# Selection shares with the queries on the partitions, small transfers on ScalarE's queue, key loads behind the queries

## The chip, the core and the metric

The kernel runs on one core of a Trainium2 chip. The core has five engines that run side by side and wait for each other by semaphores: TensorE (PE, matrix products and transposes, with its weight loads shown as PEld), VectorE (DVE), ScalarE (ACT), GpSimd (POOL) and SyncE (SP, which here only issues transfers). SP and ACT each have a queue of their own for transfers; both feed the same 16 DMA engines. Every engine runs its instructions in order. The metric is the device time in microseconds, median over runs.

## The reference

One step of a decoder layer: an RMS norm and a joint input projection, then two groups of heads side by side (native sparse attention, and a gated DeltaNet recurrence over 16 chunks of 128 tokens), then the output projection. There are 2048 prompt tokens and 8 x 4 sample tokens, 8 query heads in 2 key/value groups, head size 64. The part that the change touches is the choice of blocks in the sparse attention: probabilities over 127 compressed keys are summed into 32 blocks and over the four heads of a group, and the 8 best blocks are attended to.

```python
s = jnp.einsum('bqhgd,bchd->bhgqc', q_raw, ck).astype(jnp.float32) * scale
p = jax.nn.softmax(jnp.where(cmask, s, MASK_VALUE), axis=-1) * cmask
o_cmp = jnp.einsum('bhgqc,bchd->bqhgd', p.astype(cv.dtype), cv)
overlap = jnp.maximum(ov, 0).astype(jnp.float32) / CMP_LEN
imp = jnp.einsum('bhgqc,cn->bhqn', p, overlap)
imp = jnp.where(blk <= q_blk[:, None], imp + FORCE_BONUS * forced, MASK_VALUE)
_, idx = lax.top_k(imp, n_sel)
```

The chosen blocks then have their own softmax over rotated keys (`o_slc`), a window of 512 keys a third one (`o_win`), and the three are mixed by gates.

## The kernel before, in words

`project` computes the projections in 3-pass split precision, `gdn` the recurrence with the compression of keys as filler, `nsa` the sparse attention, and an output projection follows. Instructions are traced in the order of the code, but a planner with a simulated timeline sets the order on every engine and queue. So the work of `nsa` for its first unit is interleaved with the last steps of `gdn`, and transfers can be issued in another order than in the code.

**Projection of the keys.** For each of 5 groups of 416 tokens the keys are turned to rows in four pieces (`tk`, L406), copied by ACT to `er` (L408, two buffers under the tag `cx`) and written out (L411, L414) from SP's queue.

**The recurrence.** Step `n` of `recur` makes, in turn, `pk`, `pqs`, `pv`, `pS` (state update by DVE, L829) and `po` (L833). `tokens` loads `v` (one buffer) and `kq` for each step from SP's queue.

**Units of the sparse attention.** A unit is 512 queries of one key/value group: 4 x 2 = 8 units, in `units`. `stream` makes a unit's scores and values item by item (`pss` L1445/1446, exponential on ACT L1487, `O` L1578). Beside it the loop at the end of `nsa` advances `prepare` of the next unit at a rate that finishes in time; it also calls `load_q` for the next unit and, at units 0, 2 and 4, `load_k` for the keys of the next 512 (seven transfers, together 2.3 MB, behind the matmul `here[0]`). `QHL` and `QHM` hold the queries per group, so those of the next unit can only be loaded when the unit before the running one has used them up; `QRM` and `QRL` hold the unrotated queries and exist once.

**`prepare`** has two lists. `A` makes the compressed scores and the choice: `cmax` (row maxima from `psc`, L1321), `cmax_end` (maxima turned to rows by `rows_of`, and sent into row 97 of `QRM`), `csc` (probabilities `pT`, keys on the partitions, queries on the free axis), `share` (sums over keys by a matmul with ones, `psl` L1337; sent to DRAM, `Ld`, L1339, and read back 16 to a partition, L1341), `inverse` (reciprocal on DVE, L1344; to DRAM, L1346, and back, L1347), `share2` (block sums `psp` L1353 times the reciprocals), `select` (`psi`, sum over heads and turn, L1359; the 8 best) and `sel_rows` (mask rows into `QHM`, and a copy to the three other heads, L1372). `B` makes the exact maxima of the block and window scores (`smax`, `psm` L1379; `wmax`, `psw` L1394; `wmax0`). Both are interleaved: after entry `j` of `A`, `(j + 1) / n` of `B` has been emitted; `gap` entries of `A` only make room. `max_end` and `max_rows` close a unit with the maxima's rows in `QHM`, which the unit's own `pss` reads.

Most transfers of `nsa` go through the helper `dma` (shown as L1218) or `nc.sync.dma_start`, both SP's queue. `next_windows` copies two caches of 2 MB from DRAM to DRAM on ACT's queue at the start of units 2 and 4 (L1209).

Of the kernel before, what the change touches and what calls it, by code (L numbers as in the profile page):

```python
# [104 lines left out]
class K:  # L105
# [105 lines left out]
    def project(self):  # L211
        nc, tc, i, o = self.nc, self.tc, self.i, self.o
        with ExitStack() as st:
# [178 lines left out]
            for g in range(NG):  # L392
                gs = slice(g * GW, (g + 1) * GW)
                kr = ev.tile([128, 2, GW], F32, tag="kr", name="kr", bufs=3)
                for j in range(2):
                    ps = fm(*kw[j], g)
                    nc.scalar.activation(kr[:, j, :], ps, AF.Copy)
                    if j == 0:
                        rope(kr[:, 0, :], g, True)
                    hi, lo = hilo(kr[:, j, :])  # L400
                    nc.sync.dma_start(self.kh[:, 32 * j:32 * j + 32, gs], hi)
                    nc.sync.dma_start(self.kl[:, 32 * j:32 * j + 32, gs], lo)
                for c in range(4):
                    tp = pt.tile([128, 2, 128], F32, tag="tp", name="tk")
                    for j in range(2):
                        nc.tensor.transpose(tp[:104, j, :], kr[:, j, 104 * c:104 * c + 104], self.ident)  # L406
                    e = ev.tile([128, 256], F32, tag="cx", name="er")
                    nc.scalar.activation(e[:104].rearrange("p (c j d) -> p j c d", c=4, j=2), tp[:104].rearrange("p j (c d) -> p j c d", c=4), AF.Copy)  # L408
                    t0 = g * GW + 104 * c
                    t1 = min(t0 + 104, SEQ)  # L410
                    nc.sync.dma_start(tok(6)[t0:t1, :], e[0:t1 - t0, 0:128])  # L411
                    a = max(t0, 1536)
                    if a < t1:
                        nc.sync.dma_start(tok(10)[a - 1536:t1 - 1536, :], e[a - t0:t1 - t0, 128:256])  # L414
                    if t1 < t0 + 104:
                        nc.sync.dma_start(tok(7), e[t1 - t0:104, 0:128])
                        nc.sync.dma_start(self.wks, e[t1 - t0:104, 128:256])
# [219 lines left out]
    def gdn(self):  # L637
        nc, tc, i, o = self.nc, self.tc, self.i, self.o
        with self.gst as st:
# [143 lines left out]
                nc.scalar.activation(Y[0:64, :, 64:128], pq[:, 1], AF.Copy, scale=-1.0)  # L783

            kqr, kd4, vb4, O4, ZS = {}, {}, {}, {}, {}

            FB, FS, FL, FR = self.fills

# [18 lines left out]
            def recur(n):  # L807
# [22 lines left out]
                po = bank([128, 4, 128], "po")  # L830
                O4[n] = (self.gp if n % 2 else wk).tile([128, 4, 128], F32, tag="o4", name="o4", bufs=1)
                for h in range(4):
                    nc.tensor.matmul(po[:, h, :], QK[n][:, h, :], V[:, h, :], start=True, stop=True)  # L833
                    nc.vector.scalar_tensor_tensor(O4[n][:, h, :], ob[:, h, :], ed[:, h, n:n + 1], po[:, h, :], op0=ALU.mult, op1=ALU.add)
                yield

# [374 lines left out]
    def nsa(self):  # L1211
        nc, tc, i, o = self.nc, self.tc, self.i, self.o
        with ExitStack() as st:
# [4 lines left out]
            dma = lambda t, s, at=None: self.behind(nc.sync.dma_start(t.bitcast(F32), s), at)  # L1218
            units = [(qs, h) for qs in self.nsa_blocks for h in range(2)]
            nq = units[-1][0] + 1  # L1220

# [80 lines left out]
            def prepare(u):  # L1302
# [15 lines left out]
                def cmax(s):  # L1318
                    ps = X([128, 4, 128], "psc")
                    for g in range(4):  # L1320
                        nc.tensor.matmul(ps[:, g, :], QRM[0:97, g, 128 * s:128 * s + 128], CXL[0:97, h, 0, qs, :], start=True, stop=True)  # L1321
                    nc.vector.tensor_reduce(out=m[:, :, s], in_=ps, axis=AX.X, op=ALU.max)

                def cmax_end():
                    nc.vector.tensor_scalar(m, m, -(2.0 ** 60), -1.0, op0=ALU.max, op1=ALU.mult)
                    dma(QRM[97:98], rows_of(m.rearrange("p g s -> p (g s)"), 16))

                def csc(g):
                    ps = X([128, 512], "psr") if (qs, h) == units[0] else pS.tile([128, 512], F32, tag="s", name="psr")
# [2 lines left out]

                def share():

                    ps = X([128, 512], "psl")
                    for g in range(4):
                        nc.tensor.matmul(ps[32 * g:32 * g + 32, :], self.ones[:, 0:32], pT[g], start=True, stop=True, tile_position=(0, 32 * g))  # L1337
                    nc.vector.tensor_scalar(rl, ps, 1e-30, None, op0=ALU.max)
                    nc.sync.dma_start(u["Ld"][0], rl[0:128:32, :])  # L1339
                    u["r16"] = ns.tile([128, 16], F32, tag="r16", name="r16", bufs=1)  # L1340
                    nc.sync.dma_start(u["r16"], u["Ld"][0].rearrange("g (a x) -> (g a) x", x=16))  # L1341

                def inverse():
                    nc.vector.reciprocal(u["r16"], u["r16"])  # L1344
                    d = self.dram.tile([4, 512], F32, name="rd")
                    nc.sync.dma_start(d.rearrange("g (a x) -> (g a) x", x=16), u["r16"])  # L1346
                    nc.sync.dma_start(rl, d.unsqueeze(1).to_broadcast([4, 32, 512]))  # L1347

                def share2():

                    ps = X([128, 512], "psp")
                    for g in range(4):
                        nc.tensor.matmul(ps[32 * g:32 * g + 32, :], self.ovl, pT[g], start=True, stop=True, tile_position=(0, 32 * g))  # L1353
                    nc.vector.tensor_tensor(out=rl, in0=ps, in1=rl, op=ALU.mult)

                def select():
                    ps = X([128, 4, 32], "psi")
                    for s in range(4):
                        nc.tensor.matmul(ps[:, s, :], rl[:, 128 * s:128 * s + 128], self.gsum, start=True, stop=True)  # L1359
                    nc.vector.tensor_tensor(out=imp, in0=ps, in1=bon, op=ALU.add)  # L1360
                    t8 = ns.tile([128, 4, 8], F32, tag="t8", name="t8")
                    for s in range(4):
                        nc.vector.max(t8[:, s, :], imp[:, s, :])
                        nc.vector.match_replace(imp[:, s, :], t8[:, s, :], imp[:, s, :], 1e30)
                    nc.vector.tensor_scalar(imp, imp, 1e29, -BIG, op0=ALU.is_lt, op1=ALU.mult)

                def sel_rows():
                    tp = X([32, 512], "tsel")
                    for s in range(4):
                        nc.tensor.transpose(tp[:, 128 * s:128 * s + 128], imp[:, s, :], self.ident)  # L1370
                    nc.scalar.activation(QHM[64:96, 0], tp, AF.Copy)
                    nc.sync.dma_start(QHM[64:96, 1:4].bitcast(F32), QHM[64:96, 0:1].bitcast(F32).to_broadcast([32, 3, 512]))  # L1372

                def smax(s, g, a):
                    qt = 4 * qs + s
                    b = min(a + 4, qt + 1)
                    diag = b == qt + 1
                    ps = X([128, 512], "psm")
                    nc.tensor.matmul(ps[:, 0:128 * (b - a)], QHL[:, g, 128 * s:128 * s + 128], key(KHH, 0, h, a, b), start=True, stop=not diag)  # L1379
# [31 lines left out]
                    nc.vector.tensor_scalar(wm, wm, -1.0, None, op0=ALU.mult)  # L1411

                def max_rows():
                    dma(QHM[96:98], rows_of(wm.rearrange("p a g s -> p (a g s)"), 32))

                gap = lambda n: [None] * n
                A = [lambda s=s: cmax(s) for s in range(4)] + [cmax_end] + gap(8) + [lambda g=g: csc(g) for g in range(4)]
                A += [share] + gap(5) + [inverse] + gap(7) + [share2] + [select] + gap(2) + [sel_rows]
                B = []
                for s in range(4):  # L1420
                    for g in range(4):
# [5 lines left out]
                for j, f in enumerate(A):  # L1427
                    if f:
                        f()
                        yield  # L1430
                    e = (j + 1) * len(B) // n
                    for f in B[k:e]:
                        f()
                        yield
# [4 lines left out]
                max_rows()  # L1439
                yield  # L1440

            prepare.steps = lambda u: 16 + 32 + 16 * u["qs"] + (4 if u["qs"] else 0)
# [174 lines left out]
            here = [None]  # L1617
            for what, k in stream():
                if k in copies:
                    self.next_windows(*copies.pop(k), here[0])  # L1620
                if gen is None and k + 1 < len(units) and k + 1 not in U:
                    U[k + 1] = load_q(*units[k + 1])
                    if k % 2 == 0 and units[k][0] + 1 < nq:
                        load_k(units[k][0] + 1, here[0])
                    gen = prepare(U[k + 1])
                    done, steps, total = 0, 0, prepare.steps(U[k + 1]) + self.nx
                    rate = total / max(1, count(units[k][0]) - self.ny)
# [15 lines left out]
    mc = 9.0, 0.0  # L1643
    npre = 1
    jpre = 0
    nx, ny, npt, nos = 10, 4, 8, 9
    nd = 2, 3, 5, 8
    nb = 1.1, 0.5
# [411 lines left out]
```

## Time and profile before

| | |
|---|---|
| median of 3 runs | 2344.72 us (2339.41 to 2345.8) |
| profiled execution | 2345.71 us, span 2343.6 us |
| granted TensorE clock, mean | 0.957 of full speed |
| PE busy | 2179.5 us, 93% |
| DVE busy | 1278.6 us, 55% |
| ACT busy | 796.1 us, 34% |
| POOL busy | 766.4 us, 33% |
| transfers | 248.12 MB, of which 194.53 MB on SP's queue (q1) and 17.72 MB on ACT's (q10) |

Times in the trace are us from the span's start. A matmul in single precision shows as two records, each with a weight load. Matmuls are pipelined and their ends are modelled, so a busy PE is not PE at its peak. [...] The projections lie in about 0 to 790, the recurrence in 790 to 1216 (with the first unit's preparation in its last part), the stream of the sparse attention in 1216 to 2050, and the rest behind that.

### The profile page before, as it was taken

The numbers are of one execution on the slowest core, as the hardware profiler recorded it, in microseconds if no ns is written. First come the engines' busy times: TensorE is split into PE (matmuls) and PEld (weight loads), VectorE is DVE, ScalarE is ACT, GpSimd is POOL, SyncE is SP. The second block draws the span as 40 slices with busy tenths as digits, with TensorE's granted clock in tenths as the row PEclk, the third lists the DMA queues.
The fourth block names the chain that finished last, engine by engine and source line by source line (L and its number), as shares of the span: only waits on it lengthen the run. The fifth ranks groups of instructions, "written<-read, shape, count | busy, mean of one in ns | idle before, by whom it ended". The sixth has DMA issues, their size and how long they took to land. (4 is left out here: it accounts for less than half of the span.)

```text
span 2343.6 us, 36127 instructions
## 1 busy us (share of the span) xinstructions
PE 2179.5 (93%) x13339; PEld 1667.9 (71%) x13340; DVE 1278.6 (55%) x2660; ACT 796.1 (34%) x1688; POOL 766.4 (33%) x957
## 2 busy tenths in 40 slices
PE   6999999999999999996798969969999999999998
PEld 6999889999999788996674534535455553477765
DVE  5200246656420376566545758857778786845532
ACT  5311233332222143443353223324343434522221
POOL 4023211111200105413142334536473655422742
PEclk9999999999999899998798979989999998999999
DMA  7342421233541655437545433242222002374552
GB/s 214 108 109 62 119 86 63 77 63 73 148 141 63 187 153 157 146 106 164 133 117 97 102 76 80 51 113 48 38 48 37 21 9 57 108 229 153 195 188 93
DMA packets 304467, 248.12 MB, mean 106 GB/s; under 512 B 106039, under 2 KB 260835, under 8 KB 301987
## 3 DMA queue, kind: packets, MB, share of 16 engines
q1 hardware_dynamic: 282923, 194.53, 32.2%
q0 software_dynamic: 7424, 33.56, 4.3%
q10 hardware_dynamic: 13944, 17.72, 2.5%
q8 instruction: 105, 1.72, 0.3%
q14 instruction: 71, 0.58, 0.1%
HBM read 173.60 MB, written 74.42 MB: 106 GB/s over the span
## 5 line engine op out<-in xcount | busy, mean ns | idle before, releaser
L1588 POOL TENSOR_TENSOR pt<-pt 128x512 f32<-128x512 f32 (+3 forms) x332 | 320.5, 977 | 372.9 <-PE O L1578 160.5
L1487 ACT ACTIVATE pt<-pss 128x512 f32<-128x512 f32 (+3 forms) x544 | 254.5, 494 | 369.6 <-PE pss L1446 195.1
L1578 PE MATMUL O<-pt,V 128*64 128x512 f32 (+3 forms) x1088 | 242.9, 526 | 10.3 <-DVE pt L1497 10.3
L1382 DVE TENSOR_REDUCE bm<-psm 128x8 f32<-128x512 f32 (+3 forms) x320 | 189.6, 603 | 93.2 <-PE psm L1379 79.2
L1445 PE MATMUL pss<-qhl,khh 128*128 128x512 f32 (+3 forms) x544 | 218.5, 407 | 1.2 <-ACT pt L1487 0.6
L1445 PEld LDWEIGHTS pss<-qhl,khh 128*128 128x128 f32 x544 | 105.2, 194 | 137.5 <-issue 98.0
L1446 PE MATMUL pss<-qhm,klm 98*128 98x512 f32 (+3 forms) x544 | 192.5, 362 | 4.1 <-DMA qhl<-rl 3.8
L261 PE MATMUL ps<-xhi,whi 128*128 128x416 f32 x880 | 190.0, 357 | 0.0
L261 PE MATMUL ps<-xhi,wlo 128*128 128x416 f32 x880 | 189.7, 355 | 0.0
L261 PE MATMUL ps<-xlo,whi 128*128 128x416 f32 x880 | 187.1, 353 | 0.0
L261 PEld LDWEIGHTS ps<-xhi,whi 128*128 128x128 f32 x880 | 166.1, 190 | 13.0 <-issue 4.7
L1379 PE MATMUL psm<-khh,qhl 128*128 128x512 f32 (+3 forms) x320 | 128.7, 415 | 45.2 <-DMA qhl<-ql 26.1
L261 PEld LDWEIGHTS ps<-xhi,wlo 128*128 128x128 f32 x880 | 165.6, 189 | 2.0
L261 PEld LDWEIGHTS ps<-xlo,whi 128*128 128x128 f32 x880 | 165.4, 189 | 2.1
L1497 DVE TENSOR_TENSOR pt<-pt,caps 128x128 f32<-128x128 f32 x349 | 139.8, 419 | 20.0 <-ACT pt L1487 18.7
L1588 DVE TENSOR_TENSOR pt<-pt 128x512 f32<-128x512 f32 (+3 forms) x148 | 122.5, 837 | 38.2 <-PE O L1578 20.0
L466 DVE SCALAR_TENSOR_TENSOR acc<-cx,wc,acc 128x416 f32<-128x416 f32 (+1 forms) x180 | 123.9, 689 | 4.6
L1379 PEld LDWEIGHTS psm<-khh,qhl 128*128 128x128 f32 x320 | 62.1, 198 | 82.7 <-issue 45.6
L1446 PEld LDWEIGHTS pss<-qhm,klm 98*128 98x128 f32 x544 | 106.8, 197 | 15.2 <-DMA qhl<-rl 4.6
L1578 PEld LDWEIGHTS O<-pt,V 128*64 128x64 f32 x1088 | 55.5, 137 | 85.0 <-issue 33.3
L239 DVE TENSOR_TENSOR wlo<-wraw,whi 128x1024 fp32r<-128x1024 f32 x30 | 36.5, 1254 | 143.2 <-ACT whi L238 94.8
L1396 DVE TENSOR_REDUCE ww<-psw 128x1 f32<-128x512 f32 (+3 forms) x128 | 80.9, 632 | 28.6 <-PE psw L1395 28.0
(506 smaller groups left out, 4148.7 us busy)
## 6 DMA issues: line engine op xcount, KB each, us to landing
kq<-qkvt SPq DMA_DIRECT2D x64, 256.0 KB
qkvt<-acc SPq DMA_DIRECT2D x60, 208.0 KB
wraw<-w_in SPq DMA_DIRECT2D x24, 512.0 KB
xt<-x_prompt SPq DMA_DIRECT2D x16, 512.0 KB
m<-mx SPq DMA_DIRECT2D x16, 512.0 KB
x<-x_prompt ACTq DMA_DIRECT2D x16, 512.0 KB
out<-y SPq DMA_DIRECT2D x16, 512.0 KB
qh<-hi SPq DMA_DIRECT2D x20, 208.0 KB
```

The source lines that it names most:

```text
L239: nc.vector.tensor_tensor(out=wlo[:, :, c:c + m], in0=raw, in1=whi[:, :, c:c + m].bitcast(F32), op=ALU.subtract)
L261: nc.tensor.matmul(ps, x, y, start=(k == 0), stop=(k == 23))
L466: nc.vector.scalar_tensor_tensor(acc[:, :n], cx[:, j:j + n], wc[:, j, c:c + 1], acc[:, :n], op0=ALU.mult, op1=ALU.add)
L1379: nc.tensor.matmul(ps[:, 0:128 * (b - a)], QHL[:, g, 128 * s:128 * s + 128], key(KHH, 0, h, a, b), start=True, stop=not diag)
L1382: nc.vector.tensor_reduce(out=bm[:, s, g, 2 * a:2 * b], in_=ps[:, 0:128 * (b - a)].rearrange("p (n k) -> p n k", k=64), axis=AX.X, op=ALU.max)
L1396: nc.vector.tensor_reduce(out=ww[:, g, s, 0:1], in_=ps[:, 0:128 * (e - a)], axis=AX.X, op=ALU.max)
L1445: nc.tensor.matmul(ps, lhs1, r1, start=True, stop=False)
L1446: nc.tensor.matmul(ps, lhs2, r2, start=False, stop=True)
L1487: last = nc.scalar.activation(pt[:, c0:c1], ps[:, c0:c1], AF.Exp)
L1497: last = nc.vector.tensor_tensor(out=x, in0=x, in1=caps[:, int(nm == "neglow")], op=ALU.min)
L1578: mm = nc.tensor.matmul(O[64 * gg:64 * gg + 64, c0:c1], val, W[j][gg][:, c0:c1], start=(n == 0), stop=(n == N - 1), tile_position=(0, 64 * ...
L1588: (nc.gpsimd if e == "p" else nc.vector).tensor_tensor(out=acc[gg][:, c0:c1], in0=acc[gg][:, c0:c1], in1=W[j][gg][:, c0:c1], op=ALU.add)
```

## The change

Four things are edited. The shares are made with the queries on the partitions: `pT` slices become the stationary side against the block overlap, DVE sums the 32 block shares of a head (each key's overlaps add up to one, so this is the softmax sum), takes the reciprocal, multiplies, and sums over heads; the sums still go to `Ld` for the final merge, by a transpose and a copy in `share_rows`. The rows of maxima, the copies of the mask and the key rows in `project` are issued by ACT. `load_k` is called 8 events of the stream later (`kd`), and entries of `B` start after entry 6 of `A` (`bs`). The first `psc` is ordered behind the recurrence's `po` of step 6 and the first `psm` behind that of step 7 (`pst`), in order only, without a wait.

```diff
-                    nc.sync.dma_start(tok(6)[t0:t1, :], e[0:t1 - t0, 0:128])
+                    nc.scalar.dma_start(tok(6)[t0:t1, :], e[0:t1 - t0, 0:128])
...
-                        nc.sync.dma_start(tok(10)[a - 1536:t1 - 1536, :], e[a - t0:t1 - t0, 128:256])
+                        nc.scalar.dma_start(tok(10)[a - 1536:t1 - 1536, :], e[a - t0:t1 - t0, 128:256])
...
+                        mm = nc.tensor.matmul(ps[:, g, :], QRM[0:97, g, 128 * s:128 * s + 128], CXL[0:97, h, 0, qs, :], start=True, stop=True)
+                        if (qs, h, s, g) == (*units[0], 0, 0):
+                            self.tc.add_manual_dep(mm.ins, self.po[self.pst].ins.name, mybir.DependencyInfo(mybir.DependencyClass.NoSync, mybir.DependencyReason.DATA), reason="not ahead of its data")
...
-                    dma(QRM[97:98], rows_of(m.rearrange("p g s -> p (g s)"), 16))
+                    dma(QRM[97:98], rows_of(m.rearrange("p g s -> p (g s)"), 16), e=nc.scalar)
...
-                    ps = X([128, 512], "psl")
+                    ps = X([128, 4, 4, 32], "psp")
                     for g in range(4):
-                        nc.tensor.matmul(ps[32 * g:32 * g + 32, :], self.ones[:, 0:32], pT[g], start=True, stop=True, tile_position=(0, 32 * g))
...
+                        for s in range(4):
+                            nc.tensor.matmul(ps[:, s, g, :], pT[g][:, 128 * s:128 * s + 128], self.ovl, start=True, stop=True)
+                    u["l"] = ns.tile([128, 2, 4, 4], F32, tag="r16", name="r16", bufs=1)
+                    l, r = u["l"][:, 0], u["l"][:, 1]
+                    nc.vector.tensor_reduce(out=l, in_=ps.rearrange("p s g b -> p g s b"), axis=AX.X, op=ALU.add)
+                    nc.vector.tensor_scalar(l, l, 1e-30, None, op0=ALU.max)
+                    nc.vector.reciprocal(r, l)
+                    t = rl.rearrange("p (s g b) -> p s g b", s=4, g=4)
+                    nc.vector.tensor_tensor(out=t, in0=ps, in1=r.rearrange("p g s -> p s g").unsqueeze(3).to_broadcast([128, 4, 4, 32]), op=ALU.mult)
+                    nc.vector.tensor_reduce(out=imp, in_=t.rearrange("p s g b -> p s b g"), axis=AX.X, op=ALU.add)
+
+                def share_rows():
+                    tp = X([16, 128], "tl")
+                    nc.tensor.transpose(tp, u["l"][:, 0].rearrange("p g s -> p (g s)"), self.ident)
+                    r = ns.tile([32, 128], F32, tag="rows", name="lrows")
+                    nc.scalar.activation(r[:16], tp, AF.Copy)
+                    nc.sync.dma_start(u["Ld"][0].rearrange("g (s q) -> (g s) q", q=128), r[:16])
 
                 def select():
-                    ps = X([128, 4, 32], "psi")
-                    for s in range(4):
-                        nc.tensor.matmul(ps[:, s, :], rl[:, 128 * s:128 * s + 128], self.gsum, start=True, stop=True)
-                    nc.vector.tensor_tensor(out=imp, in0=ps, in1=bon, op=ALU.add)
+                    nc.vector.tensor_tensor(out=imp, in0=imp, in1=bon, op=ALU.add)
...
-                    nc.sync.dma_start(QHM[64:96, 1:4].bitcast(F32), QHM[64:96, 0:1].bitcast(F32).to_broadcast([32, 3, 512]))
+                    nc.scalar.dma_start(QHM[64:96, 1:4].bitcast(F32), QHM[64:96, 0:1].bitcast(F32).to_broadcast([32, 3, 512]))
...
-                    dma(QHM[96:98], rows_of(wm.rearrange("p a g s -> p (a g s)"), 32))
+                    dma(QHM[96:98], rows_of(wm.rearrange("p a g s -> p (a g s)"), 32), e=nc.scalar)
...
-                A += [share] + gap(5) + [inverse] + gap(7) + [share2] + [select] + gap(2) + [sel_rows]
+                A += [share] + gap(2) + [select] + gap(2) + [sel_rows, share_rows]
...
-                    e = (j + 1) * len(B) // n
+                    e = max(0, j - self.bs) * len(B) // (n - 1 - self.bs)
...
+                if coming:
+                    coming[0] -= 1
+                    if coming[0] < 0:
+                        load_k(coming[1], here[0])
+                        coming = None
...
-                        load_k(units[k][0] + 1, here[0])
+                        coming = [self.kd, units[k][0] + 1]
...
+    bs = 6
+    pst = 6
+    kd = 8
```

`smax` gets the same kind of order on its first matmul, behind `self.po[self.pst + 1]`; `self.po[n]` is the last `po` matmul of step `n`.

## Rows read from the trace of the kernel before

**Rows 1.** Waits of PE over the span: total us, times, longest us.
```profile
PE psm L1379 <- DMA qhl<-ql: 26.1, 4, 16.1
PE psm L1379 <- DMA mx<-mg: 16.0, 1, 16.0
PE psc L1321 <- DMA QRM<-qh: 14.8, 1, 14.8
PE pS L828 <- DVE S L829: 13.5, 2, 13.2
...
PE O L1578 <- DVE pt L1497: 10.3, 11, 3.6
PE psr L1446 <- DMA QRM<-rows: 9.7, 1, 9.7
PE tk L406 <- ACT er L408: 5.8, 2, 4.9
PE th L430 <- ACT er L408: 5.3, 2, 5.1
...
PE pss L1446 <- DMA qhl<-rl: 3.8, 1, 3.8
```
**Rows 2.** Stretches: length, busy us by engine, granted clock, DMA share, GB/s.
```profile
1077.60:1085.00 7.40, 7.38 (x44) 6.85 (x45) 3.03 (x7) 1.94 (x7) 0.77 (x3) 0.58 0.83 162
1144.10:1162.50 18.40, 18.39 (x103) 14.32 (x104) 10.90 (x37) 4.51 (x17) 1.31 (x5) 0.51 0.29 87
1249.00:1254.00 5.00, 5.00 (x17) 3.32 (x19) 1.70 (x4) 2.35 (x5) 0.00 (x0) 0.50 0.08 5
1369.50:1381.50 12.00, 12.00 (x40) 6.89 (x41) 4.11 (x11) 3.48 (x7) 1.76 (x2) 0.53 0.14 26
...
1055.00:1162.00 107.00, 75.53 (x674) 63.57 (x674) 57.47 (x175) 32.54 (x117) 24.30 (x44) 0.79 0.68 149
```
**Rows 3.** SP's queue in order of time: start, length, line, transfer, count.
```profile
1130.31 0.56 SPq L1339 DMA_DIRECT2D Ld<-rl  x1
...
1142.08 0.34 SPq L1341 DMA_DIRECT2D r<-Ld  x1
...
1245.40 0.61 SPq L1218 DMA_DIRECT2D QRM<-rows  x1
...
1338.08 1.38 SPq L1218 DMA_DIRECT2D khh<-kh  x2
...
1361.16 0.30 SPq L1218 DMA_DIRECT2D qhl<-ql  x1
...
1547.39 6.64 SPq L1250 DMA_DIRECT2D V<-svd  x1
```
**Rows 4.** DVE in order of time, in brackets the idle time and its releaser.
```profile
1143.63 0.25 DVE L1344 RECIPROCAL r<-r 128x16 f32<-128x16 f32 x1 [14.49 <-DMA r<-Ld]
```
**Rows 5.** ACT in order of time, its issues of transfers as ACTq.
```profile
1237.07 0.27 ACT L1290 ACTIVATE rows<-tm 16x128 fp32r<-16x128 f32 x1 [2.75 <-PE tm L1288]
...
1337.80 0.73 ACTq L1209 DMA_DIRECT2D out<-cache_win_k  x1
```
**Rows 6.** PE in order of time, neighbours of one line merged.
```profile
1248.78 1.65 PE L1446 MATMUL psr<-QRM,cxl 98*128 98x512 f32 x3 [9.66 <-DMA QRM<-rows]
...
1268.24 1.07 PE L1353 MATMUL psp<-pc,ovl 128*32 128x512 f32 x8
...
1271.35 1.08 PE L1359 MATMUL psi<-gsum,rl 128*128 128x32 f32 x8 [0.75 <-DVE rl L1354]
```
**Rows 7.** Instructions on `psi` and `psl`: ns min/median/max, first and last start.
```profile
L1359 PEld LDWEIGHTS psi<-gsum,rl x64: 186/192/333, 1155.2 to 1916.7; 128*128 128x128 f32 x64
...
L1338 DVE TENSOR_SCALAR rl<-psl x8: 677/684/692, 1120.4 to 1875.7; 128x512 f32<-128x512 f32 x8
```
**Rows 8.** DMA queues from 1340 to 1344: packets, MB, share of 16 engines.
```profile
q10 hardware_dynamic: 81, 1.32, 82.3%
q1 hardware_dynamic: 36, 0.07, 4.8%
```

More of the change, by code (lines that the diff above doesn't have):

```diff
@@ L785, in gdn @@
             kqr, kd4, vb4, O4, ZS = {}, {}, {}, {}, {}
+            self.po = {}
             FB, FS, FL, FR = self.fills
@@ L832, in recur @@
                 for h in range(4):
-                    nc.tensor.matmul(po[:, h, :], QK[n][:, h, :], V[:, h, :], start=True, stop=True)
+                    self.po[n] = nc.tensor.matmul(po[:, h, :], QK[n][:, h, :], V[:, h, :], start=True, stop=True)
                     nc.vector.scalar_tensor_tensor(O4[n][:, h, :], ob[:, h, :], ed[:, h, n:n + 1], po[:, h, :], op0=ALU.mult, op1=ALU.add)
@@ L1217, in nsa @@
             pM = st.enter_context(self.pool(name="pnM", bufs=self.pb3[2], space=PSUM))
-            dma = lambda t, s, at=None: self.behind(nc.sync.dma_start(t.bitcast(F32), s), at)
+            dma = lambda t, s, at=None, e=nc.sync: self.behind(e.dma_start(t.bitcast(F32), s), at)
             units = [(qs, h) for qs in self.nsa_blocks for h in range(2)]
@@ L1320, in cmax @@
                     for g in range(4):
-                        nc.tensor.matmul(ps[:, g, :], QRM[0:97, g, 128 * s:128 * s + 128], CXL[0:97, h, 0, qs, :], start=True, stop=True)
+                        mm = nc.tensor.matmul(ps[:, g, :], QRM[0:97, g, 128 * s:128 * s + 128], CXL[0:97, h, 0, qs, :], start=True, stop=True)
+                        if (qs, h, s, g) == (*units[0], 0, 0):
+                            self.tc.add_manual_dep(mm.ins, self.po[self.pst].ins.name, mybir.DependencyInfo(mybir.DependencyClass.NoSync, mybir.DependencyReason.DATA), reason="not ahead of its data")
                     nc.vector.tensor_reduce(out=m[:, :, s], in_=ps, axis=AX.X, op=ALU.max)
@@ L1333, in share @@
                 def share():
-                    ps = X([128, 512], "psl")
+                    ps = X([128, 4, 4, 32], "psp")
                     for g in range(4):
-                        nc.tensor.matmul(ps[32 * g:32 * g + 32, :], self.ones[:, 0:32], pT[g], start=True, stop=True, tile_position=(0, 32 * g))
-                    nc.vector.tensor_scalar(rl, ps, 1e-30, None, op0=ALU.max)
-                    nc.sync.dma_start(u["Ld"][0], rl[0:128:32, :])
-                    u["r16"] = ns.tile([128, 16], F32, tag="r16", name="r16", bufs=1)
@@ L1341, in share @@
[L1341 to L1354, printed above, removed]
+                        for s in range(4):
+                            nc.tensor.matmul(ps[:, s, g, :], pT[g][:, 128 * s:128 * s + 128], self.ovl, start=True, stop=True)
@@ L1378, in smax @@
                     ps = X([128, 512], "psm")
-                    nc.tensor.matmul(ps[:, 0:128 * (b - a)], QHL[:, g, 128 * s:128 * s + 128], key(KHH, 0, h, a, b), start=True, stop=not diag)
+                    mm = nc.tensor.matmul(ps[:, 0:128 * (b - a)], QHL[:, g, 128 * s:128 * s + 128], key(KHH, 0, h, a, b), start=True, stop=not diag)
+                    if (qs, h, s, g) == (*units[0], 0, 0):
+                        self.tc.add_manual_dep(mm.ins, self.po[self.pst + 1].ins.name, mybir.DependencyInfo(mybir.DependencyClass.NoSync, mybir.DependencyReason.DATA), reason="not ahead of its data")
                     if diag:
@@ L1440, in prepare @@
                 yield
-            prepare.steps = lambda u: 16 + 32 + 16 * u["qs"] + (4 if u["qs"] else 0)
+            prepare.steps = lambda u: 15 + 32 + 16 * u["qs"] + (4 if u["qs"] else 0)
             def scores(ps, lhs1, lhs2, r1, r2):
@@ L1616, in nsa @@
             gen, nxt, done, total = None, None, 0, 0
-            here = [None]
+            here, coming = [None], None
             for what, k in stream():
```

## The prediction

> **What bounds the kernel now.** I read the busy times first: TensorE (PE) is busy 2179.5 of the span's 2343.6 us, so at most 164 us can come from its idle time, and a faster engine elsewhere gives nothing by itself. Next, the waits of PE, longest in total [rows 1]: about half of that idle time stands in a few long waits, nearly all for data that the diff touches. [...] Last, the queue of SyncE (SP) and the engine in front of PE [rows 3, 4, 5], because a wait that is named after a transfer can be one for the transfer's turn. The profiled execution took 2345.71 us, 1 us over the median of 2344.72; the sum is made against 2345.71.
>
> The waits by stage, all from rows 1: **A**, in the projection of the keys (5.8 + 5.3, `tk` and `th` for `er`); **B**, the first compressed maximum for its queries (14.8); **C**, the shares' round trip (13.2 of 13.5, in one piece); **D**, the masks (3.6) and the maxima's row (9.7); **E**, the two long waits at unit changes with key loads (16.0 and 16.1); **F**, the short ones at the other changes (26.1 - 16.1 = 10.0 for `qhl`, and 3.8 for `pss`).
>
> **The change part by part.**
>
> *A: key rows leave by ScalarE's queue (L411, L414).* `er` shares two buffers, and ACT can't fill one before its transfer has left; PE then waits for ACT. Issued by ACT, the transfer follows the copy at once instead of SP's other work. Stake: 11.1 us, and about 2 us of half clock behind each of the two waits (an estimate from the 5 us at 0.50 in rows 2): 15. Price: some 26 more issues on ACT; the one ACT issue that I have a row for took 0.73 us [rows 5], 19 us on an engine two thirds idle. Bounds 0 and 15; I take 11, since the transfer has only to land a few us earlier.
>
> *C: the shares with the queries on the partitions.* Before, the sums went to DRAM (issued 1130.31) and came back (issued 1142.08), and DVE stood 14.49 us at the reciprocal, ahead of the recurrence's state update, for which PE waited 13.2 us [rows 1, 3, 4]. Now sum and reciprocal follow PE with no transfer between. That wait goes, and with it 18.4 us at 0.51, worth 9.0 [rows 2].
>
> *B: the first `psc` is kept behind the recurrence's step 6, the first `psm` behind step 7 (`pst`).* Stake 14.8, plus 7.4 us at 0.58, worth 3.1. But nothing is loaded less here. B and C lie in one stretch, 1055 to 1162, whose DMA share is 0.68 over 107 us [rows 2]: 73 us of transfers if they ran gapless, against PE's 75.5 busy us less 12 for the clock. So of the 40.1 us of B and C no more than 107 - 73 = 34 can come back. What is late next is the recurrence's own `v`, single-buffered and in the same queue. Bounds 10 (little more than the clock's part) and 34; I take the middle, 22.
>
> *D: key loads later, the row of maxima by ACT's queue.* The masks were loaded behind the second keys; with these out of the way the 3.6 go. The row was ready at 1237.07 + 0.27, SP came to it at 1245.40, and PE had it at 1248.78, 3.4 us after that issue [rows 3, 5, 6]. From ACT: 1237.3 + 0.73 + 3.4 = 1241.4, so 7.4 of the 9.7 come back, with half of the 5 us at 0.50 behind them [rows 2]: 3.6 + 7.4 + 2.5 = 13.5. I take 13; bounds 7 and 18.
>
> *E: key loads eight steps later, behind the queries.* At 1338.08 the keys go into SP's queue, and the last piece of the queries' block tile follows at 1361.16 [rows 3]; PE stands until 1369.5 [rows 2]. Afterwards the queries follow as soon as their buffer is free, and the mask and maxima rows go by ACT's queue. Stake: 32.1, plus 12 us at 0.53 behind each, worth 5.6 twice [rows 1, 2]: 43.3. What stays: the row of maxima is made last in a unit and needs 0.73 + 3.4 us, of which a few `psc` cover perhaps one; I leave 3 us of waiting and 3 us of clock at each: 43.3 - 12 = 31. Bounds 20 (half is met again at the row) and 43.3. The deferred keys are needed a unit later and move beside matmuls; if they were late, the unit after would wait for them as this one did for queries.
>
> *F: block maxima six entries later (`bs`).* Four `psc` and a step or two of the stream now stand between a unit's change and the first matmul on its queries, about as long as these waits (10.0 us over three, and 3.8). Stake 13.8 [rows 1] and about 2 us of half clock behind each of four (an estimate, as in A): 22. I take 13; bounds 7 and 22.
>
> *What PE gets more of.* Before, a unit had `psl` and `psp`, both of one form, 8 records in 1.07 us each, and `psi`, 8 records of 128 x 32 in 1.08 [rows 6]: 3.2 us. Now 16 matmuls of the form of `psi`, 32 records, four times 1.08: 4.3, and one transpose (0.15, an estimate from the same spacing). That is +1.25, in eight units 10 us, and PE is the bound, so it counts in full. A weight load of `psi` took 192 ns [rows 7]; if the loads did not overlap, a unit would need 32 x 0.192 = 6.1 us, and the addition would be 25. The rows show them overlapped (1.08 / 8 = 0.135 a record); I take 10. [...]
>
> *What the others get.* DVE: a unit has two passes over 512 elements (0.684 us as `rl<-psl` [rows 7]) and small ones more or less, under 1.5 us on an engine 55% busy, all behind PE's own work. ACT: 24 issues at 0.73, 17.5 us, beside a busy share of 34%. Bounds 0 and 17.5; I take 4, for exponentials that come a little later.
>
> Sum: 11 + 22 + 13 + 31 + 13 = 90, less 10 and 4: **76 us**. 2345.7 - 76 = 2269.7, so **2270 us**.
>
> **The rivals.**
>
> *R1: the small transfers still wait behind the large ones.* From the issue of the shares' sums to that of the next step it took 1142.08 - 1130.31 = 11.8 us, behind queries just issued [rows 3]. If ACT's transfers take as long, the row in D lands at 1249.8 (-10), and those in E some 12 us after they are made (-11 at each): 76 - 32 = 44, 2302 us. Against it: from 1340 to 1344 ACT's queue held 82.3% of the DMA engines and SP's 4.8%, with SP's keys already issued [rows 3, 8]; it does not stand behind SP's. [...]
>
> *R2: every wait goes with its half clock.* 15 + 34 + 18 + 43.3 + 22 - 14 = 118: 2228 us. For it: each wait has one clear cause in the rows. Against it: E and D keep a chain of transpose, copy and transfer, and B and C would need transfers without a gap.
>
> *R3: it doesn't do what it says.* The order on an engine comes from a planner with its own times. If the first `psm` stays where it was, F gives nothing (-13), and if unit 0 just waits at the next load, B and C give 10 (-12): 51, 2295 us. For it: the planner placed a `psc` 14.8 us too early.
>
> *R4: slower, ACT blocked.* An issue on a full queue holds its engine: one value load held SP 6.64 us [rows 3]. If each of 24 issues held ACT so long, ahead of exponentials that PE waits for, that is 159 us against 90 - 10 = 80: 2425 us. It decides from 80 / 24 = 3.3 us an issue. Against it: ACT's issue at 1337.80 took 0.73 us [rows 5].
>
> **How the numbers follow.** Forecast 0.54, R1 0.16, R2 0.11, R3 0.10, R4 0.09. Only R4 is slower. Within 0.3% (7 us, about what a measurement tells from no change) I put 0.03, taken from R1 and R3 at their worst. So faster 0.88, same 0.03, slower 0.09. The range goes from 2234, close to R2, to 2318, R1 and most of R3 together; outside are R4, half of R2 and a strip of R1, under 0.2.
>
> **What would show it.** C: no wait of DVE for `r<-Ld`, none of 13 us for `pS`. B: `psc` waits under 4 us, and `v` or `kq` do not take its place. E and F: no wait above 5 us at a unit's change, and the clock at 1.00 through it. D: `psr` waits under 3 us. The shares of a unit in 4 to 5 us of PE. Wrong would be waits of 8 us or more for `qhm` (R1), a first `psm` that waits as before (R3), ACT issues above 3 us (R4), or a new wait for keys at the next unit.

## The result, and the profile after

The changed kernel takes 2305.11 us (median of 4 runs, 2303.0 to 2310.85) beside 2344.79 for the kernel before: ratio 0.9839, 95% interval 0.9816 to 0.9863. That is 40 us faster where 76 were forecast; the time lies inside the range, 35 us above the number.

I split the span of each profiled execution in three: PE's idle time (span less PE busy); the time lost at half clock (half of PE's busy time inside the stretches at 0.50; in the kernel after, a `psm` matmul of 128x512 took 775 ns in the median there and 401 elsewhere); and work, which is the rest.

| us | span | PE idle | lost at 0.50 | work |
|---|---|---|---|---|
| before | 2343.6 | 164.1 | 63.3 | 2116.2 |
| after | 2301.7 | 111.3 | 63.6 | 2126.8 |
| difference | -41.9 | -52.8 | +0.3 | +10.6 |

So the waits went, the added work came as forecast, and the clock that the forecast counted with them, some 22 of its 90 us (each term's share of half clock, cut as the term was), did not come back. First the waits of PE after, in the form of [rows 1]: total us, times, longest.

```profile
PE pss L1447 <- DMA qhm<-rows: 14.7, 5, 5.5
PE pst L801 <- DMA v<-qkvt: 14.1, 3, 11.6
...
PE tk L406 <- ACT er L408: 7.3, 5, 2.6
...
PE pqs L817 <- ACT oT L917: 4.0, 1, 4.0
...
PE th L430 <- ACT er L408: 2.5, 2, 1.5
```

The two waits of 16 us for queries, the one of 13 for the state update and the one of 9.7 for the row of maxima [rows 1] are gone; `v` and the maxima's rows have come in their place. Next PE in order of time, at the shares of two units, and stretches around them (columns as in [rows 2]: length, busy us of PE, PEld, DVE, ACT, POOL, then the granted clock):

```profile
1388.30 4.40 PE L1341 MATMUL psp<-ovl,pc 128*128 128x32 f32 x32
...
1718.05 3.65 PE L1341 MATMUL psp<-ovl,pc 128*128 128x32 f32 x32
```

```profile
1380.00:1388.30 8.30, 8.30 (x47) 4.59 (x45) 7.15 (x14) 2.87 (x8) 5.71 (x6) 1.00 1.02 190
1388.30:1391.20 2.90, 2.90 (x28) 2.90 (x26) 2.29 (x4) 1.17 (x3) 2.19 (x3) 1.00 0.43 125
1391.20:1398.00 6.80, 6.80 (x25) 4.25 (x24) 3.21 (x7) 0.49 (x1) 1.32 (x2) 0.50 0.18 53
...
1718.00:1722.30 4.30, 4.30 (x38) 4.02 (x36) 0.66 (x2) 0.00 (x0) 1.90 (x2) 1.00 0.02 4
1722.30:1732.50 10.20, 10.20 (x36) 6.31 (x36) 8.49 (x20) 1.55 (x6) 2.79 (x6) 0.50 0.00 0
```

Read the PE column against the length: PE is busy without a gap before, in and behind the shares, and yet the granted clock falls to 0.50 of full speed at the end of the 32 records (1.5 us ahead of it in the first unit shown, 0.6 behind it in the second). Before, PE had idled 1.3 us or more in the 12 us ahead of every such stretch but one (0.3 us, at 923.4 in the recurrence); here it has idled 0.00 and 0.02 us ahead of the two falls shown. The records themselves are as cheap as forecast (3.65 us in most units, against the 4.3 worked out from [rows 6]).

### The profile page after: what moved, and what is told of

Read it like the earlier page. It is cut to its first block, busy times and chain, and to the rows that moved or that the text cites. A ratio compares the mean times of both kernels' runs of the same rounds, so it can differ in the third digit from the quotient of the medians.

```text
span 2301.7 us, 36249 instructions
## 1 busy us (share of the span) xinstructions
PE 2190.3 (95%) x13412; PEld 1688.9 (73%) x13412; DVE 1290.7 (56%) x2684; ACT 799.2 (35%) x1696; POOL 763.8 (33%) x949
## 4 chain that ended last, share of the span: by engine, by line
PE 76%; DMA 11%; DVE 7%; issue 2%; ACT 2%; POOL 1%; SPq 1%; ACTq 0%; POOLq 0%; DVEq 0%
PE ps L261 18%; PE O L1579 8%; PE ps L249 8%; PE ps L1977 6%; PE pss L1446 5%; PE u L1177 4%; PE pss L1447 4%; PE psm L1378 3%; DMA v<-qkvt 2%; DMA qhm<-rows 1%; PE psw L1395 1%; PE psp L1341 1%; PE psg L701 1%; PE tp L1162 1%; DMA out<-er 1%
## 5 line engine op out<-in xcount | busy, mean ns | idle before, releaser
L1589 POOL TENSOR_TENSOR pt<-pt 128x512 f32<-128x512 f32 (+3 forms) x323 | 314.1, 984 | 336.0 <-DVE pt L1498 145.5
L1447 PE MATMUL pss<-qhm,klm 98*128 98x512 f32 (+3 forms) x544 | 193.5, 365 | 14.7 <-DMA qhm<-rows 14.7
L261 PEld LDWEIGHTS ps<-xhi,whi 128*128 128x128 f32 x880 | 166.7, 192 | 16.3 <-issue 4.8
L1589 DVE TENSOR_TENSOR pt<-pt 128x512 f32<-128x512 f32 (+3 forms) x157 | 128.6, 828 | 30.7 <-PE O L1579 14.9
L237 POOL TENSOR_TENSOR wraw<-wraw,wn 128x1024 f32<-128x1024 f32 x28 | 54.7, 1955 | 104.9 <-DMA wraw<-w_in 63.5
```

What stands on the lines that cost most here:

```text
L261: nc.tensor.matmul(ps, x, y, start=(k == 0), stop=(k == 23))
L1447: nc.tensor.matmul(ps, lhs2, r2, start=False, stop=True)
L1589: (nc.gpsimd if e == "p" else nc.vector).tensor_tensor(out=acc[gg][:, c0:c1], in0=acc[gg][:, c0:c1], in1=W[j][gg][:, c0:c1], op=ALU.add)
```

## The experiments

Each was timed in five rounds beside the kernel before; the ratio is to that kernel's runs, and can differ from the ratio of the two medians by 0.001, some 3 us. "Behind the shares" is PE time lost at 0.50 from the first record of `psp` in a unit to 8 us behind the last, summed over the eight units. The last four columns are of one traced run for each kernel; it took 11 us more than the median in e1, 8 in e10 and 6 in e11, 20 less in e7 and 6 less in e9, and elsewhere lies within 5.

| | median us (runs from to) | ratio to before, 95% | idle | lost at 0.50 | work | behind the shares |
|---|---|---|---|---|---|---|
| after | 2305.1 (2303 to 2311) | 0.9839 (0.9816 to 0.9863) | 111.3 | 63.6 | 2126.8 | 12.2 |
| e1 key rows on SP | 2312.5 (2301 to 2323) | 0.9842 (0.9818 to 0.9866) | 116.9 | 81.8 | 2123.0 | 16.3 |
| e2 old shares | 2330.7 (2327 to 2341) | 0.9940 (0.9917 to 0.9962) | 138.3 | 61.3 | 2127.0 | 0.9 |
| e3 keys at once | 2346.7 (2337 to 2352) | 0.9991 (0.9975 to 1.0007) | 145.6 | 77.1 | 2123.8 | 19.4 |
| e4 small ones on SP | 2311.7 (2308 to 2315) | 0.9845 (0.9826 to 0.9865) | 112.8 | 68.1 | 2132.6 | 15.8 |
| e5 shares split | 2315.6 (2306 to 2319) | 0.9865 (0.9842 to 0.9888) | 119.9 | 70.6 | 2125.3 | 17.0 |
| e6 two buffers for v | 2301.8 (2298 to 2305) | 0.9815 (0.9797 to 0.9833) | 108.0 | 67.6 | 2126.6 | 8.5 |
| e7 bs undone | 2327.8 (2308 to 2335) | 0.9936 (0.9915 to 0.9958) | 122.5 | 60.8 | 2123.1 | 11.7 |
| e8 ny 8 | 2321.0 (2308 to 2326) | 0.9891 (0.9868 to 0.9914) | 108.3 | 89.8 | 2125.8 | 22.4 |
| e9 shares turned | 2295.6 (2290 to 2298) | 0.9787 (0.9766 to 0.9808) | 126.1 | 50.9 | 2111.2 | 2.7 |
| e10 e9 and two v | 2292.1 (2280 to 2301) | 0.9764 (0.9736 to 0.9792) | 128.8 | 59.9 | 2109.6 | 3.1 |
| e11 before, new shares | 2355.1 (2348 to 2366) | 1.0040 (1.0022 to 1.0058) | 149.2 | 91.2 | 2119.3 | 20.2 |
| e12 before, turned shares | 2323.7 (2315 to 2327) | 0.9894 (0.9872 to 0.9916) | 160.8 | 60.2 | 2104.7 | 0.6 |

**e1.**
```diff
-                    nc.scalar.dma_start(tok(6)[t0:t1, :], e[0:t1 - t0, 0:128])
+                    nc.sync.dma_start(tok(6)[t0:t1, :], e[0:t1 - t0, 0:128])
```
(and the same for `tok(10)`.) 

> The changed kernel with the key rows of the projection issued by SP again (the only edit). Theory 1 (the transfer out of er waits for its own landing, not for SP's turn, so moving its issue gave nothing): no slower than the changed kernel, 2300 to 2306 us; tk and th together wait about as long for er as in the changed kernel (7.3 + 2.5 us). Rival, the forecast's term: 11 us slower, about 2316, with the waits back at 5 us each.

The ratio is that of the changed kernel, 0.9842 to 0.9839, so A gave nothing measurable (the medians, each against the kernel before beside it, make it 5 us, inside the error). But PE's two waits of 5 us for `er` are back, as the rival has it:

```profile
PE tk L406 <- ACT er L408: 6.9, 2, 5.6
...
PE th L430 <- ACT er L408: 5.2, 2, 5.0
```

ACT's waits for the transfers out of `er` (total, times, longest), in the changed kernel and then in this one:

```profile
ACT er L408 <- DMA out<-er: 29.6, 15, 5.5
```

```profile
ACT er L408 <- DMA out<-er: 35.2, 10, 10.8
```

By ACT's queue a few long waits become many short ones, 6 us less on ACT and 2 us less on PE (9.8 instead of 12.1). Two buffers still wait for the landing, 29.6 us on ACT.

**e2.** In `share` to `select` the code of before, with its gaps in `A`. 

> The changed kernel with the shares made as before (sums by ones, round trip through DRAM, three small products), all else changed. Theory 2 (the 32 records of 128x32 in a row, 3.65 us a unit, make the granted clock fall behind them: 12.2 us of PE time lost at 0.50 behind five of the eight): the half-clock stretches that stand behind a share without any idle time of PE go, so 12 us come back, PE's busy time falls by a further 3 or so, and the wait of 13 us in the recurrence for the round trip returns with about 5 us of clock: 2300 to 2312, about the same time. Rival, the forecast's terms (22 of B and C, less 10): slower by 12 or more, 2317 and up, and the stretches at half clock stay where they are, since they would come from something else.

Slower by 0.0101, 24 us: the rival's size, and against Theory 2's "about the same". The rival's other half is not there: of the 12.2 us behind the shares 0.9 are left, from a fall 19 us ahead of them. But the whole loss at 0.50 is nearly that of the changed kernel (61.3 and 63.6), so new waits spent what the old form saved. DVE's waits for the round trip in this kernel, and in the one before:

```profile
DVE r L1347 <- DMA r<-Ld: 34.1, 5, 13.7
```

```profile
DVE r L1344 <- DMA r<-Ld: 16.9, 5, 14.5
```

Among the other edits DVE waits twice as long for the round trip as it did before, and the forecast had priced it for unit 0 alone. Whether that is because the key loads, now later, meet it was not tested. Theory 2 needed a test without the round trip (e9, e11, e12).

**e3.**
```diff
-                        coming = [self.kd, units[k][0] + 1]
+                        load_k(units[k][0] + 1, here[0])
```


> The changed kernel with the second, third and fourth key loads called at once again instead of 8 events later. Theory: the queries stand behind 2.3 MB of keys again, two waits of some 16 us for the queries return at the changes to units 2 and 4, and the rows that wait there now (4.4 and 5.5 us) are covered by them: +25, about 2330. Rival: the maxima's row, by its own queue, is late anyway, and the keys only take its place: +10 or less, 2305 to 2315.

0.9991: nearly the whole gain goes, 36 us, where 25 were expected; idle time of PE grows by 34. The two waits of 16 us come back in pieces: PE idles 18.9 us from 1330 to 1400 and 13.4 from 1540 to 1600, under several names. Among the new waits:

```profile
PE tm L1289 <- ACT T L1508: 10.9, 1, 10.9
...
PE psr L1447 <- DMA QRM<-rows: 8.5, 1, 8.5
PE psm L1378 <- DMA qhl<-ql: 7.3, 2, 5.5
```

The wait for the row of compressed maxima (D) is back although ACT still issues it. ACT in order of time, this row made and issued:

```profile
1234.49 0.27 ACT L1291 ACTIVATE rows<-tm 16x128 fp32r<-16x128 f32 x1 [2.01 <-PE tm L1289]
1240.15 0.57 ACTq L1219 DMA_DIRECT2D QRM<-rows  x1
```

Nothing stands between the two on ACT, and yet the issue comes 5.4 us after the row. On SP in those microseconds:

```profile
1230.13 5.80 SPq L1251 DMA_DIRECT2D V<-wvd  x1
1235.97 4.00 SPq L1517 DMA_DIRECT2D gt<-gts  x2
```

The first of them is the last of the key loads. ACT issues the row right behind the second, so its queue seems to have been held up with SP's; what held it, the profile does not show.

**e4.**
```diff
-                    dma(QRM[97:98], rows_of(m.rearrange("p g s -> p (g s)"), 16), e=nc.scalar)
+                    dma(QRM[97:98], rows_of(m.rearrange("p g s -> p (g s)"), 16))
```
(and the same for `max_rows` and the copies of the mask.) 

> The changed kernel with the three small transfers of the preparation (row of compressed maxima, copies of the mask, rows of exact maxima) back on SP's queue. Theory: each row waits for SP's turn behind the queries just issued, 8 us at unit 0 and some 5 to 10 us at five changes: +25, about 2330. Rival (R1 of the forecast: issuer does not matter, transfers share the engines): within 5 us of the changed kernel.

Within the error of the changed kernel; the rival was right (`pss` waits 18.3 us for its rows, against 14.7). In the queue of SP, and on PE, of this kernel:

```profile
1226.14 0.59 SPq L1219 DMA_DIRECT2D QRM<-rows  x1
```

```profile
1228.10 1.63 PE L1447 MATMUL psr<-QRM,cxl 98*128 98x512 f32 x3
```

The row was ready at 1226.1, SP issued it at once, and `psr` followed without a wait. With e3: what freed this row was the key load that went, not the other queue.

**e5.** Four entries `part(g)` with one head's 8 records each, in place of the 32 in `share`. 

> The changed kernel with the 32 records of the shares not in a row: one head's 8 at a time, with a step of the stream, and behind the first and the third head a block maximum, between them. Theory 2, now on four profiles of the 32 records in a row (22 of 32 shares with a stretch at 0.50 behind them and no idle time ahead; 12 to 19 us of PE time lost a run): the stretches behind the shares go and 10 to 16 us come back, 2290 to 2297. Rival: the stretches come from the records' number, not from their standing together, or from other work there: no change, 2302 to 2312.

No gain, where 10 to 16 us were expected, but no fair test either. (Of the 22 shares that the expectation counts, three had 1 to 3.5 us of idle time ahead.) PE's order in one unit:

```profile
1501.31 2.80 PE L1340 MATMUL psp<-ovl,pc 128*128 128x32 f32 x22
1503.92 0.77 PE L1381 MATMUL psm<-khh,qhl 128*128 128x512 f32 x1
1504.50 1.75 PE L1340 MATMUL psp<-ovl,pc 128*128 128x32 f32 x8
```

The planner set 22 of the 32 in a row again. Unit by unit the traces say more: the clock fell behind all four units in which 20 to 24 stayed in a row, and behind one of the four with 16 or fewer. And `psi` of the kernel before and of e2 is 8 records of this form in a row: in 16 units no fall began between its first record and 8 us behind its last. Where fewer stood together the fall was rarer; with four units on each side that is a sign and not a proof.

**e6.**
```diff
-                v = wk.tile([128, 4, 128], F32, tag="v", name="v", bufs=1)
+                v = wk.tile([128, 4, 128], F32, tag="v", name="v", bufs=2)
```


> The changed kernel with two buffers for the recurrence's v, so that a step's v is loaded a step earlier; the order on all engines but SP is the same. Theory 3 (B's wait only moved from the first psc to v because v has one buffer and its load is late in the queue): the waits of pst for v (11.7 + 1.9 us) go; what is late next is what lies behind in the same queue, and half of it is met again: -6 to -14, 2291 to 2299. Rival (the limit of 73 us of transfers against PE's work in that stretch): another load takes the whole wait over, no change.

The wait for `v` went, and this came in the same place, as the rival had it; 3 us less idle, 0.0024 of the ratio, inside the error:

```profile
PE pqs L817 <- ACT oT L917: 10.3, 1, 10.3
```

In this stretch 10 to 15 us of waiting stay, whichever load is named: `psc` before [rows 1], `v` after, `oT` here.

**e7.**
```diff
-                    e = max(0, j - self.bs) * len(B) // (n - 1 - self.bs)
+                    e = (j + 1) * len(B) // n
```


> The changed kernel with the block maxima spread over the preparation as before (bs undone). Forecast's term F: +13, with the waits of the first psm for the queries back at the changes without key loads (4 to 6 us at three). Theory 4 (the four psc cover the queries, but then the maxima's row is waited for at the same change, 14.7 us over five): what psm waits for now is time the row would be waited for anyway: +0 to +6.

PE's waits:

```profile
PE psm L1378 <- DMA qhl<-ql: 11.6, 4, 4.9
...
PE pss L1447 <- DMA qhm<-rows: 9.4, 3, 5.3
```

The queries are waited for again and the rows less, as Theory 4 has it, but 11 us more are idle in all and the kernel is 23 us slower, where Theory 4 allowed 6 and the forecast 13. The traced run is of 2308 us, 20 under the median, and shows only the 11. For the rest there is the clock: every run has its span and granted clock on record, and span times (1 - clock) is the time that the clock took from it, idle time at 0.50 counted in. That is 93 us here in the mean of six runs and 79.5 in the changed kernel's four; in the traced run it was 71.5.

**e8.** `ny` 8 instead of 4. 

> The changed kernel with the preparation ending 8 instead of 4 stream steps before the unit's end, so that the maxima's rows leave earlier. Theory 4 (the row chain of transpose, copy, issue and landing takes 5 to 10 us and is made last): most of the 14.7 us of waits for the rows goes, with a few us of half clock: -8 to -18, 2287 to 2297. Rival: the block maxima then press on DVE earlier, and PE waits for exponentials and masks instead: 0 to +8.

The rows are waited for half as long (7.6 instead of 14.7 us), yet the kernel is 12 us slower by the ratios (16 by the medians), more than the rival's 8. In the traces, 22 us apart, idle is -3, work -1, lost at 0.50 +26. Of that 10 stand behind the shares. Why most of the rest fell in units 0 to 2 is not settled; the 7 us of waits did not show as a gain.

**e9.**
```diff
-                    ps = X([128, 4, 4, 32], "psp")
+                    ps = X([128, 512], "psp")
                     for g in range(4):
-                        for s in range(4):
-                            nc.tensor.matmul(ps[:, s, g, :], pT[g][:, 128 * s:128 * s + 128], self.ovl, start=True, stop=True)
+                        nc.tensor.matmul(ps[32 * g:32 * g + 32, :], self.ovl, pT[g], start=True, stop=True, tile_position=(0, 32 * g))
+                    nc.scalar.activation(rl, ps, AF.Copy)
+
+                def share2():
+                    ps = X([128, 4, 4, 32], "psq")
+                    for s in range(4):
+                        nc.tensor.transpose(ps[:, s].rearrange("p g b -> p (g b)"), rl[:, 128 * s:128 * s + 128], self.ident)
```


> The changed kernel with the shares made by the overlap as the stationary side (8 records of 128x512 a unit, the form of the old psp), copied by ACT and turned to the queries by four transposes; everything behind that, and all else, as in the changed kernel. The transfer-free path stays, the form of 32 records of 128x32 goes. Theory 2 (that form costs the clock behind it): in seven profiles of that form in a row 8 to 22 us of PE time were lost at 0.50 behind the shares; these go, and with them 3.65 - 1.07 - 0.6 = 2 us of PE work in each of eight units: -16 and -8 to -20, so 2270 to 2285. Rival (the stretches belong to what else stands there, as the run with the split shares would have it): only the work, -10 to -16, 2290 to 2297, with stretches at 0.50 behind the shares as before; or less, if PE then waits for the copy.

PE at the shares of a unit of this kernel, and the stretch around them:

```profile
1487.03 1.07 PE L1340 MATMUL psp<-pc,ovl 128*32 128x512 f32 x8
...
1492.40 0.66 PE L1346 MATMUL psq<-ident,rl 128*128 128x128 f32 x4
```

```profile
1480.00:1500.00 20.00, 19.17 (x114) 11.60 (x113) 18.80 (x41) 5.44 (x15) 11.73 (x16) 1.00 0.12 40
```

The clock stays at 1.00. Against the changed kernel work falls by 15.6 us (8 x 2.0 were expected) and the loss at 0.50 by 12.7; idle time grows by 15, in many places (the rows 19.3 instead of 14.7 us, the exponentials 4 more); that it is the same data awaited by a PE that comes sooner is likely, but was not tested. So 12 us come back by the ratios, 13 by the traces, of the 28 of the two savings. The time is thus the rival's (2290 to 2297) and not the theory's; but the stretches behind the shares are gone, which the rival denied, and what ate the gain is waiting. The granted clock of all runs agrees: span times (1 - clock) is 66.5 us here in the mean, 13 under the changed kernel's.

**e10.** Both edits of e9 and e6. 

> The same with two buffers for v. With v in two buffers alone the wait for v went and one of 10.3 us for oT took its place in the same stretch; 3 to 4 us came back. Expected here the same again: 3 to 4 us under the kernel with the turned shares alone. Rival: none of it, within 2 us.

0.0023 under e9, as e6 is 0.0024 under the changed kernel; each is inside the error. It is the fastest kernel here, 55 us ahead of the kernel before and 18 of the changed one by their ratios.

**e11.** The kernel before with the change's `share`, `share_rows` and `select` alone. 

> The kernel before with the new shares alone (queries on the partitions, no round trip, its mask copy and rows on SP's queue as before). Forecast's terms for C and what PE gets more of: 13.2 + 9 - 10 = -12, 2333. Theory 5 (the shares and the later keys need each other: without the later keys the changed kernel keeps 2 us of its 40, with the old shares 14): the waits for queries behind keys stay, the clock falls behind the shares: 0 to -6, 2339 to 2346. If the two simply add: -24, 2321, what undoing the shares cost.

Slower than before by 0.4%, beyond every expectation. Idle time fell by 15 us as C promised, work grew by 3, and 28 more were lost at 0.50. The traced run has the lowest clock of its twelve (0.948, mean 0.953); for the kernel's 9 us, 21 lost would do (an estimate, 9 + 15 - 3). One share of it, on PE and in stretches:

```profile
1911.62 4.51 PE L1338 MATMUL psp<-ovl,pc 128*128 128x32 f32 x32
```

```profile
1904.00:1911.60 7.60, 7.60 (x41) 4.29 (x40) 6.81 (x14) 3.05 (x7) 4.05 (x4) 1.00 0.00 0
1911.60:1914.30 2.70, 2.70 (x27) 2.70 (x26) 1.55 (x4) 0.46 (x2) 1.84 (x4) 1.00 0.00 0
1914.30:1924.50 10.20, 10.20 (x38) 6.88 (x39) 5.64 (x12) 2.75 (x5) 0.00 (x0) 0.50 0.01 2
```

**e12.** The kernel before with the shares of e9 alone. 

> The kernel before with the turned shares alone (overlap stationary, 8 records of 128x512, copy, four transposes; no round trip). With the shares in the form of the change alone the kernel before got 9 us slower: 15 us less idle time of PE, 3 more of work, and 28 more of PE time lost at 0.50, 20 of it behind the shares. Theory 2 (it is the form, not the missing round trip): idle 15 us less again, work some 12 to 15 less, the time lost at 0.50 within 8 of before's 63: 2310 to 2325. Rival (the clock fell for another reason, for example that the work behind is placed otherwise): the loss at 0.50 again 20 us or more above before's, 2335 and up.

The same path without the form: 0.9894, 25 us faster than before and 34 faster than e11. A unit's shares, stretch:

```profile
1745.00:1765.00 20.00, 19.48 (x112) 11.87 (x112) 18.18 (x42) 6.33 (x16) 7.34 (x13) 1.00 0.04 10
```

The loss at 0.50 is 60.2, three under before's, and 31 under that of e11, with nothing edited between the two but the form of the shares, and the copy and turn that belong to it. By the clock of all runs the two kernels are 16 us apart (span times (1 - clock): 110 and 94), so e11's trace shows too much; work makes 15 of the 34. The time is as expected; the idle time is not, it fell by 3 and not by 15: other waits filled in (32.5 us of `psm` for queries, against 26.1 [rows 1]). With e9 this shows Theory 2, in two settings: the half clock behind the shares comes with that form (12.2 us in the changed kernel, 20.2 in e11) and goes with it (2.7 in e9, 0.6 in e12). Which part of the form does it, the 32 moving columns, the weight load of 128 ahead of each or the number in a row, was not told apart.

## Why the prediction was right in its direction and half right in its size

Of the 90 us forecast some 68 were idle time and 22 clock. The traces are 42 us apart where the sum was 76. Of the 34 that are missing, 15 are idle time that stayed or came up elsewhere, 12 are lost clock behind the shares, 10 are other clock that did not come back, and 1 is work; the balance is the 4 that the sum took off for ACT, of which nothing is seen (e4, with 24 of these issues back on SP, is no faster).

**What PE gets more of, priced at 10: this step failed.** Its work was right (+10.6). Its clock was not in the sum. In the eight kernels that hold the 32 records as the change has them, the clock fell behind 42 of 64 shares (behind 37 with under 1 us of idle time in the 12 us ahead of them and among them), for 8.5 to 22.4 us a run, 15.8 in the mean. Each of the 42 falls began 2.4 to 5.6 us after a unit's first share record. The term should have been about 26, in the traced run of the changed kernel 22. I looked at the form's spacing and weight loads, and took the clock from waits alone.

**Clock behind the waits, some 22 of the 90.** At C about 7 came back (9.1 lost there before, 1.7 after). Over units 0 to 7 the loss rose from 33.4 to 38.9 us, with the shares' 12.2 among them. Without these the loss over the whole span is 12 us under before's: about half of the 22 came back, and the shares took it.

**C.** Right in mechanism: DVE's wait of 14.49 us and PE's of 13.2 are gone. Undoing it costs 24 us (e2); alone, in the change's form, it loses 9 (e11).

**B.** Of the 22 for both, B's part is zero: the 14.8 of `psc` became 11.65 for `v` and 3.99 for `oT` in the step after. The prediction named `v` as what is late next, and took back too little for it; e6 shows a third wait behind that. From the stretch of both (1050 to 1205 before, 1050 to 1200 after) 11 us of idle time and 5 of lost clock went, 16 of the 22, nearly all of it C's: that the middle of the bounds came near is luck.

**D, 13.** The row's 9.7 us went in full and the masks' 3.6 to 1.6, but the row's by another cause than the one given, so the number is right by luck: the queue did nothing (e4), and with the keys back the wait is back (e3).

**E, 31.** Near in size: undoing the later keys undoes D's row too, and costs 34 us of idle time and 36 of time (e3), of the 44 of both terms. In place of the two 16 us waits stand 0.9 and 3.0 for the rows. The clock gave less: 11.8 us were lost behind these two waits before, 8.1 at the same changes after.

**F, 13.** About 23 us, 11 of them idle and most of the rest clock (e7): more than forecast. What stays there is the row: 4.4 and 5.5 us at the changes to units 1 and 3, which the forecast had left at nothing.

**A, 11.** Nothing measurable, 2 us of waits (e1). Its lower bound was the right value: most of the wait was for the landing (9.8 of PE's 12.1 us stay with the issues on ACT).

**The rivals.** R1 came closest in number (2302), and its mechanism is there in one place. ACT's issue of the row for unit 3, PE's wait for it, and the queues from 1428 to 1440:

```profile
1428.80 0.67 ACTq L1219 DMA_DIRECT2D qhm<-rows  x1
```

```profile
1439.11 1.62 PE L1447 MATMUL pss<-qhm,klm 98*128 98x512 f32 x3 [5.51 <-DMA qhm<-rows]
```

```profile
q1 hardware_dynamic: 771, 1.41, 82.2%
q10 hardware_dynamic: 34, 0.02, 1.4%
```

It took 9.6 us from the end of its issue to its use, beside queries of SP's queue; [rows 8], from which I argued that ACT's queue goes ahead, had ACT's large copies under way and hardly anything of SP. With the key rows issued by SP (e1, ratio 0.9842) or the small transfers issued by it (e4, 0.9845) the time was that of the changed kernel (0.9839). These two runs and this row speak for R1's mechanism. The chance of 0.16 that I gave R1 looks low for its mechanism; but R1 would take 32 us, and the rows cost 14.7, so that its number came near is luck in part. R2 fell with the clock and with the waits for `v` and the rows. R3's first `psm` waits 0.7 us for queries in all, so F worked; its other half, that unit 0 just waits at the next load, came true for B. R4 fell with the issues: 0.67 us here, where it decided at 3.3.

## What to carry to other kernels

Before a product is turned round, look at which side moves: here 32 records in a row that each move 32 columns cost the clock behind them (behind 42 of 64 shares, 15.8 us a run in the mean), and the bill stands with other work, at a PE that looks fully busy. Split a change's effect into idle time, time lost at half clock and work before explaining it; here three numbers showed which term had failed. And where a wait is named after one load of a crowded stretch, ask which load is next before counting its length.

## What was not expected of the hardware

The granted clock fell to 0.50 with PE busy throughout (2.70 of 2.70 us, then 10.20 at 0.50, in e11). In these rows, and in the 7.60 us ahead of them, the profile's busy time did not show the fall coming: it was full. The kernel before has one stretch of this kind too: at 923.4 us, in the recurrence, the clock fell while 16 records of one moving column each ran (`bp`, 921.9 to 924.2), with 0.3 us of idle time ahead. Whether they did it was not tested, and why records of this form bring the fall is open.

It does not happen each time: 22 of the 64 shares had no such stretch, and the same kernel's runs lie up to 27 us apart (2308 to 2335 in e7), against 12 for the kernel before beside it (2338 to 2350). That scatter is the clock's for the most part: the granted clock was 0.969 in the run of 2308 us and 0.955 in that of 2335, which by the reckoning of e7 is 71.5 and 105 us.
